# One load queue for the front of a decoder layer, and the cache compression spread over the input projection

## The chip, the cores and the metric

The kernel runs on one core of a Trainium2 chip. The core has a matrix engine (TensorE, PE in the profile), VectorE (DVE), ScalarE (ACT), GpSimd (POOL) and SyncE (SP). Each engine takes its instructions in program order; SP, ACT and POOL also issue DMAs, which run on 16 DMA engines. The metric is the device time of one execution in microseconds (us).

## The reference

One layer of a decoder, for a prompt of 1024 tokens and for 8 batches of 8 new tokens that have a cache of past keys and values. Cut to what matters:

```python
mod = (silu(c) @ w_ada + b_ada)[:, None, :]
shift1, scale1, gate1, shift2, scale2, gate2 = split(mod, 6)
h = rms_norm(x, norm1) * (1 + scale1) + shift1
z = h @ w_in
q, kc, vc, ks, vs, kw, vw, gates, conv_bg, conv_cg, conv_h, pool_in = split(z, IN_SPLITS)
...
k_cmp = rms_norm(compress(full[:, :, 0], cmp_pe[0], cmp_w1[0], cmp_w2[0]), k_gain[0])
v_cmp = compress(full[:, :, 1], cmp_pe[1], cmp_w1[1], cmp_w2[1])
...   # three attentions (compressed, selected, window), convolution, pooling
x = x + gate1 * (concat([o_attn, y_conv, y_pool]) @ w_out)
h = rms_norm(x, norm2) * (1 + scale2) + shift2
x = x + gate2 * swiglu(h, w_up, w_down)
```

Everything is fp32. `compress` turns overlapping blocks of the past keys and values into one row each, by two small matrices (`w1`, `w2`) and a position term (`pe`).

## The kernel before

Features lie on the 128 partitions, tokens along the free dimension: 1024 prompt tokens and 64 new ones, in three chunks of 384, 384 and 320 (`CHUNKS`, line 26). Products that need fp32 accuracy are three matmuls of a high and a low part (`mm3`, line 141).

The program is written as tasks: Python generators that emit a step and yield the time, by a rough clock of the engines, from which their next step can run (`run`, line 83). The order in which steps are emitted, with some freedom that the recording layer takes by a timeline of its own, fixes the order of every engine's queue. So a change of the tasks moves instructions on all engines. Waits are semaphores; a tile that is used again waits for its last readers.

The stages that the change touches:

- **Modulation** (`ada_rounds`, line 339). Six vectors (shift1, scale1, gate1, shift2, scale2, gate2), numbered 0 to 5. The weights of one vector come in 16 loads. Before, a round is half a vector: per step four loads of 256 KB, in pieces of 128 columns (512 B), and 16 matmuls of 128 columns on quarters of the array, accumulated over two steps, then an evacuation, a transpose and an add (line 380). Vectors 0 and 1 are made in the front, the other four (`late_ada`, line 899) during the input projection, with one step of loads ahead.
- **Norm** (`norm_load` 435, `norm_squares` 441, `modulate` 404). x comes by ScalarE's queue. Squares on ScalarE are summed over the eight feature tiles on VectorE into `n_ss`; one matmul with a matrix of 1/1024 (`mean_d`) makes the mean; then root (ScalarE) and reciprocal (VectorE, `n_rs`). Then, per feature tile, scale into a temporary `n_t`, add the shift into `h_hi` and form `h_lo`.
- **Compression** (`compress`, line 498). The cache pages come eight at a time, an octet (`compress_load`, 492: six by SP's queue and two by POOL's, into one of three `stream` tiles, one of which holds `w1`). One octet is 16 fp32 matmuls of 128 columns. Four octets are a batch; `compress_evac` and `compress_post` (575) close it with a few small matmuls (`vt,c_w`, `ksq,mean_h`, a transpose of `vcT`). The first three batches (`EARLY`) run in this stage, the other five in the attention. `compress_prompt` (549) does the same for the prompt's own keys.
- **Input projection** (`input_projection`, line 833). First the token part (`token_part`, 672): nine token tiles by the 280 columns of `wtok` (vs, vw, gates), with eight loads of `wtok` on ScalarE's queue and low parts on VectorE. Then 16 weight tiles by three chunks, 48 steps of 24 matmuls.

The front runs as one task (`front`, line 1920) at priority 1, next to the input projection at 1 and the compression at 2 (line 1986); the compression fills the time in which the other two wait. After the projection come the attention, the output projection and the feed-forward part, in which no line changes but for the names of two tiles.

Of the kernel before, what the change touches and what calls it, by code (L numbers as in the profile page):

```python
# [17 lines left out]
P = 128  # L18
# [3 lines left out]
NB = 8  # L22
# [38 lines left out]
class Kernel:  # L61
# [55 lines left out]
    def bank_of(self, tag):  # L117
        """waits for a bank of the tag"""
        while not self.free[tag] or min(self.free[tag]) > self.t["pe"]:
            yield self.ready(tag)  # L120
        return self.take(tag)

    # ---------------------------------------------------------------- helpers
    def mm(self, out, lhsT, rhs, start, stop, chain=False):
# [10 lines left out]
        self.nc.tensor.matmul(out, lhsT, rhs, start=start, stop=stop, skip_group_check=chain)  # L135
# [5 lines left out]
    def mm3(self, out, a, b, start, stop, chain=False):  # L141
        self.mm(out, a[0], b[0], start, False, chain)
        self.mm(out, a[0], b[1], False, False, chain)
        self.mm(out, a[1], b[0], False, stop, chain)
# [10 lines left out]
    def combine(self, out, a, b, op, n, ready=0.0, eng=None):  # L155
        """out = a op b in SBUF on VectorE or GpSimd, by default the one that is done first"""
# [25 lines left out]
    # ---------------------------------------------------------------- constants  # L182
# [60 lines left out]
    def constants3(self, c):  # L243
        nc = self.nc
        with self.pool("ctmp") as tp:
# [9 lines left out]
            # zeros, then the causal triangle; the window's older edge; the compressed blocks that are not over yet  # L255
# [15 lines left out]
            # row index -> token t of a sample row (b2, g, r, t)  # L271
# [7 lines left out]
            # sum over the four heads of a key group  # L279
# [12 lines left out]
            # new tokens: key (b', t') is seen by row (b, t) when b' == b and t' <= t  # L292
# [11 lines left out]
            # the oldest window keys: key k is out of the window of token t when k <= t  # L304
# [6 lines left out]
            # token partition (64 + (b, t)) -> row (b2, g, r, t) of the pair p  # L311
# [8 lines left out]
            # head of a sample row  # L320
# [10 lines left out]
    # ---------------------------------------------------------------- adaLN  # L331
# [7 lines left out]
    def ada_rounds(self, pool, rs, bufs, eng, tag, margin=0.0):  # L339
        """vectors rs of the modulation, [feature, (prompt, 8 batches)], half a vector at a time"""  # L340
        nc = self.nc
        todo = [(r, hf) for r in rs for hf in range(2)]
        steps = [(x, kh) for x in range(len(todo)) for kh in range(2)]
        W = {}

        def load(i):
            if i < len(steps):
                x, kh = steps[i]
                r, hf = todo[x]
                W[i] = []  # L350
                for g in range(4):
                    t = pool.tile([P, KT // 2, P], F32, name="wada", bufs=bufs)
                    eng.dma_start(t, self.i["wada"][r * 4 + g, :, kh * 4:kh * 4 + 4, hf * P:(hf + 1) * P])
# [5 lines left out]
        for i in range(ahead):  # L359
            load(i)  # L360
        for i, (x, kh) in enumerate(steps):
            r, hf = todo[x]
            yield W[i][4] + margin
            if kh == 0:
# [7 lines left out]
            if kh == 0:  # L372
                continue
            s = pool.tile([P, P], F32, name="ada_s", bufs=2)
            r_ = self.evac(s, acc[:, :P], P)
# [3 lines left out]
            self.tr(tr[:, :P], s)  # L379
            nc.vector.tensor_tensor(  # L380
                self.mod[:, r].rearrange("p (g j) b -> p j g b", j=2)[:, hf],
                tr[:, :P].rearrange("p (g m) -> p g m", m=32)[:, :, 0:9],
                self.bada[:, r].rearrange("p (g j) -> p j g", j=2)[:, hf][:, :, None].to_broadcast([P, 4, 9]),
                op=OP.add)
            self.give(tag, self.use("dve", 0.2, self.t["pe"]))
            if hf == 1:
                if r in (1, 4):
                    out, norm = (self.s1, self.norm1) if r == 1 else (self.s2, self.norm2)
                    nc.vector.scalar_tensor_tensor(out, self.mod[:, r], 1.0, norm[:, :, None].to_broadcast([P, KT, 9]),
                                                   op0=OP.add, op1=OP.mult)  # L390
                self.ada_at[r] = self.use("dve", 0.3, self.t["pe"]) + 0.2
# [1743 lines left out]
```

## Time and profile before

| | us |
|---|---|
| timed runs: median of 3 (lowest, highest) | 1712.49 (1708.04, 1713.7) |
| profiled execution, first to last instruction (span) | 1707.9 |
| TensorE busy | 1606.5 (94%) |
| VectorE busy | 1121.0 (66%) |
| ScalarE busy | 821.8 (48%) |
| GpSimd busy | 704.6 (41%) |

The profiled execution is one execution, taken by the hardware profiler; its span lies just under the lowest timed run. In the profile's rows L135 is the helper that records every matmul, so matmuls are told apart by their operands: `bank<-wada,sc` is the modulation, `bank<-stream` the compression, `bank<-wt_hi,h_hi` and the like the token part, `bank<-h_hi,w_hi` the projection. "PE" is the matmul, "PEld" its weight load. Idle time is given with what released it.

### The profile page before, as it was taken

What the parts mean: (1) busy time and instruction counts of PE and PEld (TensorE: products, weight loads), DVE (VectorE), ACT (ScalarE), POOL (GpSimd) and SP (SyncE); (2) the same over time, 40 slices, a digit from 0 to 9 for tenths busy, and PEclk for the clock granted to TensorE, in tenths of its full rate; (3) what the DMA queues carried; (4) which work ended last, traced back from release to release, by engine and by line L of the source; (5) the groups of instructions that cost most, each with busy time, mean ns of one, the idle gap of its engine ahead of it and who ended that gap; (6) DMA issues with size and microseconds to landing.
All of it is one profiled execution on the core that took longest, in us unless ns stands there. A gap on an engine that the chain in (4) does not pass through costs nothing.

```text
span 1707.9 us, 35277 instructions
## 1 busy us (share of the span) xinstructions
PE 1606.5 (94%) x12317; PEld 1427.7 (84%) x12317; DVE 1121.0 (66%) x2886; ACT 821.8 (48%) x1892; POOL 704.6 (41%) x812
## 2 busy tenths in 40 slices
PE   6789999997999999999799789999999999899998
PEld 5689999987877566666599779999999998889997
DVE  1491334767556867666599996555555556998887
ACT  1363212326676766766675543332333334655554
POOL 1121000003342322222206486555555555888976
PEclk9899999999999999999999989999999999999999
DMA  9854455425664644540883224225222225744433
GB/s 273 258 180 127 143 141 138 136 75 179 202 193 128 195 141 122 160 131 10 276 253 105 75 72 135 96 96 194 97 96 100 96 96 186 237 128 130 133 82 125
DMA packets 214851, 245.13 MB, mean 144 GB/s; under 512 B 25985, under 2 KB 182850, under 8 KB 214354
## 3 DMA queue, kind: packets, MB, share of 16 engines
q1 hardware_dynamic: 190546, 209.77, 40.1%
q10 hardware_dynamic: 18288, 17.01, 3.2%
q0 software_dynamic: 5840, 16.10, 2.9%
q8 instruction: 98, 1.61, 0.4%
q14 instruction: 79, 0.65, 0.1%
HBM read 202.33 MB, written 44.67 MB: 145 GB/s over the span
## 4 chain that ended last, share of the span: by engine, by line
PE 31%; DVE 9%; issue 4%; DMA 3%; POOL 3%; ACT 1%; ACTq 0%; POOLq 0%; DVEq 0%; SPq 0%
PE bank L135 31%; DVE w_lo L160 2%; DMA w_raw<-in_wup 2%; POOL w_s L160 1%; DVE b_lo L160 1%; DVE g_lo L160 1%; DVE x L1706 1%; DVE d_lo L160 1%; POOL b_t L160 1%; DMA w_raw<-in_wdown 0%; DMA mixc<-mix_d 0%; ACT w_hi L164 0%; DMA x<-x_d 0%; DVE n_ss L160 0%; POOL f_T L160 0%
## 5 line engine op out<-in xcount | busy, mean ns | idle before, releaser
L135 PE MATMUL bank<-b_lo,w_hi 128*128 128x272 f32 x1232 | 355.8, 291 | 2.7 <-DVE b_lo L160 2.5
L135 PE MATMUL bank<-b_hi,w_hi 128*128 128x272 f32 x1232 | 351.6, 292 | 6.9 <-DVE f_v L1512 3.3
L135 PE MATMUL bank<-b_hi,w_lo 128*128 128x272 f32 x1232 | 351.4, 290 | 2.1 <-DVE w_lo L160 2.1
L135 PEld LDWEIGHTS bank<-b_hi,w_hi 128*128 128x128 f32 x1232 | 232.1, 191 | 9.6 <-ACT b_hi L164 4.9
L135 PEld LDWEIGHTS bank<-b_lo,w_hi 128*128 128x128 f32 x1232 | 234.5, 190 | 4.0 <-DVE b_lo L160 3.9
L135 PEld LDWEIGHTS bank<-b_hi,w_lo 128*128 128x128 f32 x1232 | 233.0, 190 | 3.1 <-DVE w_lo L160 2.8
L160 POOL TENSOR_TENSOR w_s<-w_raw 128x512 f32<-128x512 f32 (+1 forms) x122 | 164.2, 1347 | 147.8 <-DVE w_lo L160 134.1
L1011 POOL TENSOR_SCALAR P<-P,st 128x640 f32<-128x640 f32 (+11 forms) x192 | 111.5, 591 | 241.8 <-DVE st L1009 89.5
L164 ACT ACTIVATE w_hi<-w_raw 128x512 fp32r<-128x512 f32 (+2 forms) x130 | 86.5, 676 | 176.5 <-PE bank L135 141.2
L160 DVE TENSOR_TENSOR w_lo<-w_raw,w_hi 128x512 fp32r<-128x512 f32 (+2 forms) x129 | 115.6, 904 | 83.2 <-PE bank L135 47.4
L160 DVE TENSOR_TENSOR w_lo<-w_s,w_hi 128x512 fp32r<-128x512 f32 (+1 forms) x144 | 127.4, 888 | 45.4 <-ACT w_hi L164 38.6
L135 PE MATMUL bank<-stream 128*128 128x128 f32 x1056 | 137.2, 289 | 19.4 <-DMA stream<-in_cacheA 14.5
L135 PEld LDWEIGHTS bank<-stream 128*128 128x128 f32 x1056 | 130.4, 203 | 28.5 <-issue 21.8
L160 POOL TENSOR_TENSOR x<-x,d_m 128x272 f32<-128x272 f32 x144 | 141.1, 1001 | 25.2 <-DVE x L1706 13.1
L164 ACT ACTIVATE w_hi<-w_s 128x512 fp32r<-128x512 f32 (+1 forms) x144 | 89.2, 624 | 113.2 <-PE bank L135 57.1
L135 PE MATMUL bank<-h_hi,w_hi 128*128 128x384 f32 (+1 forms) x384 | 129.4, 337 | 1.0 <-ACT py L826 1.0
L135 PE MATMUL bank<-h_hi,w_lo 128*128 128x384 f32 (+1 forms) x384 | 126.7, 330 | 0.0
L135 PE MATMUL bank<-h_lo,w_hi 128*128 128x384 f32 (+1 forms) x384 | 126.4, 329 | 0.0
L1003 ACT ACTIVATE P<-P,st 128x640 f32<-128x640 f32 (+11 forms) x192 | 113.0, 591 | 13.0 <-DVE st L994 6.5
L135 PE MATMUL bank<-g_hi,w_hi 128*128 128x272 f32 x308 | 92.0, 301 | 13.1 <-DVE x L1706 6.7
L139 PEld LDWEIGHTS bank<-ident,P 128*128 128x128 f32 (+1 forms) x592 | 64.1, 138 | 46.4 <-issue 30.2
L139 PE MATMUL bank<-ident,P 128*128 128x128 f32 (+1 forms) x592 | 95.6, 284 | 2.5 <-DVE pt L152 1.7
(363 smaller groups left out, 4111.0 us busy)
## 6 DMA issues: line engine op xcount, KB each, us to landing
wada<-in_wada SPq DMA_DIRECT2D x96, 256.0 KB, 5.2
stream<-in_cacheA SPq DMA_DIRECT2D x192, 128.0 KB, 3.1
w_raw<-in_wup SPq DMA_DIRECT2D x48, 512.0 KB, 3.9
g_raw<-g_d SPq DMA_DIRECT2D x70, 272.0 KB, 3.1
unit<-in_cacheB SPq DMA_DIRECT2D x136, 128.0 KB, 2.3
stream<-in_cacheB SPq DMA_DIRECT2D x120, 128.0 KB, 2.2
w_raw<-in_wout SPq DMA_DIRECT2D x24, 512.0 KB, 4.5
g_d<-f_T SPq DMA_DIRECT2D x84, 136.0 KB, 1.8
```

The source lines that it names most:

```text
L135: self.nc.tensor.matmul(out, lhsT, rhs, start=start, stop=stop, skip_group_check=chain)
L139: self.nc.tensor.transpose(out, in_, self.ident)
L160: (self.nc.vector if eng == "dve" else self.nc.gpsimd).tensor_tensor(out, a, b, op=op)
L164: self.nc.scalar.activation(hi, src, AF.Copy)
L1003: nc.scalar.activation(Ps, Ps, AF.Exp, scale=-1.0, bias=sy[:, 0:1], accum_out=sy[:, 1:2])
L1011: nc.gpsimd.tensor_scalar(Ps, Ps, sy[:, 3:4], 0.0, op0=OP.mult, op1=OP.add)
L1706: nc.vector.scalar_tensor_tensor(out[:, :n], acc[:, :n], self.mod[:, 5, m, 0:1], out[:, :n], op0=OP.mult, op1=OP.add)
```

## The change

SP's queue brings, in this order: x's first chunk, the 16 loads of scale1, x's second chunk, the token weights in two loads, the 16 loads of shift1, x's last chunk, then `w1` and cache pages. A load of modulation weights now takes two feature tiles by whole rows of 256 columns (2 KB in one piece per partition); a modulation matmul is 256 columns wide, and a vector is accumulated over four steps. The order of the two vectors is scale first, then shift.

For the first two chunks the mean is taken on TensorE from each feature tile's squares (eight matmuls, no sums on VectorE); the last chunk keeps the sums. x is scaled in place as soon as the scale vector is there, and the shift is added in a second pass; the new tokens' part is done for all feature tiles at once. x's second chunk lies in the tile that later takes the projected keys and values. The token weights lie in two `stream` tiles, and GpSimd forms their low parts.

The compression starts behind the token tile that ends the second chunk, and its priority is now 0.9 while octets x 30 < 12 x steps of the projection, else 2: its twelve octets are spread over the projection's first 30 steps.

```diff
     def ada_rounds(self, pool, rs, bufs, eng, tag, margin=0.0):
-        todo = [(r, hf) for r in rs for hf in range(2)]
-        steps = [(x, kh) for x in range(len(todo)) for kh in range(2)]
+        steps = [(r, kq) for r in rs for kq in range(4)]
...
-                    t = pool.tile([P, KT // 2, P], F32, name="wada", bufs=bufs)
-                    eng.dma_start(t, self.i["wada"][r * 4 + g, :, kh * 4:kh * 4 + 4, hf * P:(hf + 1) * P])
+                    t = pool.tile([P, 2, 256], F32, name="wada", bufs=bufs)
+                    self.ada_load = eng.dma_start(t, self.i["wada"][r * 4 + g, :, kq * 2:kq * 2 + 2, :])
...
-        for i in range(ahead):
-            load(i)
+        with self.tc.issue_after(self.x_load.ins):
+            for i in range(ahead):
+                load(i)
...
-            for k in range(4):
+            for k in range(2):
                 for g in range(4):
-                    self.mm(acc[32 * g:32 * g + 32, :P], self.sc[:, kh * 4 + k, :], W[i][g][:, k, :],
-                            kh + k == 0, kh + k == 4)
+                    self.mm(acc[32 * g:32 * g + 32, 0:256], self.sc[:, kq * 2 + k, :], W[i][g][:, k, :],
+                            kq + k == 0, kq + k == 4)
...
+    def norm_load(self, c, x):
+        c0, n = CHUNKS[c]
+        self.x_load = self.nc.sync.dma_start(x, self.i["xT"][:, :, c0:c0 + n])
...
+    def norm_scale(self, pool, c, rs, x, r, tag="b"):
...
+        if c == 2:
+            ss = pool.tile([P, 384], F32, name="n_ss")
+            for k in range(KT):
+                r = self.square_sum(pool, ss, x[:, k, :n], k, n, r)
...
+        else:
+            m = yield from self.bank_of(tag)
+            for k in range(KT):
+                sq = pool.tile([P, 384], F32, name="n_t", bufs=2)
+                nc.scalar.activation(sq[:, :n], x[:, k, :n], AF.Square)
...
+                self.mm(m[:, :n], self.mean_d, sq[:, :n], k == 0, k == KT - 1)
...
+    def modulate(self, c, x, hi, lo, at):
...
+        for k in range(KT):
+            t = x[:, k, :np_]
+            nc.vector.scalar_tensor_tensor(t, t, s[:, k, 0:1], rs[:, :np_], op0=OP.mult, op1=OP.mult)
...
+        yield from self.hold(lambda: 0 in self.ada_at and (c == 0 or c - 1 in self.h_done))
...
+            nc.scalar.activation(hk, t, AF.Identity, bias=sh[:, k, 0:1])
...
+            nc.vector.scalar_tensor_tensor(lk, t, sh[:, k, 0:1], hk.bitcast(F32), op0=OP.add, op1=OP.subtract)
...
     def compress_setup(self, pool):
-        nc.sync.dma_start(w1, self.i["w1"].rearrange("p v k m -> p (v k) m"))
-        for x in range(2):
-            self.compress_load(x)
+        with self.tc.issue_after(self.x_load.ins):
+            nc.sync.dma_start(w1, self.i["w1"].rearrange("p v k m -> p (v k) m"))
+            for x in range(2):
+                self.compress_load(x)
...
     def compress(self, pool, batches, ahead):
-        yield from self.hold(lambda: self.ada_loaded >= 5)
+        yield from self.hold(lambda: self.tok_last)
...
+    def token_loads(self):
+        for half in range(2):
+            raw = self.stream_tile().rearrange("p a b -> p (a b)")[:, 0:1120].rearrange("p (k m) -> p k m", k=4)
+            self.nc.sync.dma_start(raw, self.i["wtok"][:, half * 4:half * 4 + 4])
...
     def token_part(self, pool, h):
+            r = self.split(hi[:, s], lo[:, s], raw, 1120, at, "pool")
...
+            if j == 5:
+                self.tok_last = last
...
     def input_projection(self, h):
-        yield from self.hold(lambda: self.ada_done)
+        yield from self.hold(lambda: self.ada_loaded >= 8)
...
     def front(self, h):
+        def begin(pool, c, x):
+            rs = pool.tile([P, 384], F32, name="n_rs", bufs=2)
+            xs[c] = self.norm_load(c, x())
+            self.spawn(0.4 + 0.1 * c, self.norm_scale(pool, c, rs, *xs[c]))
+            self.spawn(0.4 + 0.1 * c, self.modulate(c, xs[c][0], h[c][0], h[c][1], self.h_at[c]))
...
-                ada = self.ada_rounds(ap, (0, 1), 16, self.nc.sync, "b")
+                begin(np_, 0, lambda: np_.tile([P, KT, CHUNKS[0][1]], F32, name="x0"))
+                ada = self.ada_rounds(ap, (1, 0), 16, nc.sync, "b")
+                t = next(ada)
+                x1 = self.kv.rearrange("p v t -> p (v t)")[:, 0:KT * CHUNKS[1][1]]
+                with self.tc.issue_after(self.ada_load.ins):
+                    begin(np_, 1, lambda: x1.rearrange("p (k t) -> p k t", k=KT))
+                    self.token_loads()
...
+                with self.tc.issue_after(self.ada_load.ins):
+                    begin(n2, 2, lambda: n2.tile([P, KT, CHUNKS[2][1]], F32, name="x2"))
...
     def build(self):
-        self.run((1, self.front(h)), (1, self.input_projection(h)), (2, self.compress(cp, range(EARLY), 1)))
+        early = lambda: 0.9 if self.octets * 30 < EARLY * 4 * self.z_steps else 2
+        self.run((1, self.front(h)), (1, self.input_projection(h)), (early, self.compress(cp, range(EARLY), 1)))
```

`issue_after(x)` keeps what is emitted under it behind x on its engine; `hold` waits with the emission until a condition holds. Comments that the diff drops are left out here.

More of the change, by code (lines that the diff above doesn't have):

```diff
@@ L134, in mm @@
         self.t["pe"] += cost
-        self.nc.tensor.matmul(out, lhsT, rhs, start=start, stop=stop, skip_group_check=chain)
+        return self.nc.tensor.matmul(out, lhsT, rhs, start=start, stop=stop, skip_group_check=chain)
     def tr(self, out, in_):
@@ L378, in ada_rounds @@
             tr = yield from self.bank_of(tag)
[L379 to L391, printed above, removed]
+            for j in range(2):
+                self.tr(tr[:, j * P:(j + 1) * P], s[:, j * P:(j + 1) * P])
+            for j in range(2):
+                nc.vector.tensor_tensor(
+                    self.mod[:, r].rearrange("p (g j) b -> p j g b", j=2)[:, j],
+                    tr[:, j * P:(j + 1) * P].rearrange("p (g m) -> p g m", m=32)[:, :, 0:9],
+                    self.bada[:, r].rearrange("p (g j) -> p j g", j=2)[:, j][:, :, None].to_broadcast([P, 4, 9]),
+                    op=OP.add)
+            self.give(tag, self.use("dve", 0.4, self.t["pe"]))
+            if r in (1, 4):
+                out, norm = (self.s1, self.norm1) if r == 1 else (self.s2, self.norm2)
+                nc.vector.scalar_tensor_tensor(out, self.mod[:, r], 1.0, norm[:, :, None].to_broadcast([P, KT, 9]),
+                                               op0=OP.add, op1=OP.mult)
+            self.ada_at[r] = self.use("dve", 0.3, self.t["pe"]) + 0.2
     def square_sum(self, pool, ss, x, k, n, ready, width=384, eng="dve"):
@@ L449, in compress_setup @@
+        self.h_done.add(c)
     def compress_setup(self, pool):
@@ L676, in token_part @@
         lo = pool.tile([P, KT, 280], F32R, name="wt_lo")
-        for k in range(KT):
-            raw = pool.tile([P, 280], F32, name="wt_raw", bufs=3)
-            nc.scalar.dma_start(raw, self.i["wtok"][:, k])
-            r = self.split(hi[:, k], lo[:, k], raw, 280, self.use("dma", 0.45, self.t["pe"]) + 2)
+        yield from self.hold(lambda: self.wt_raw)
+        for half, (raw, at) in enumerate(self.wt_raw):
+            s = slice(half * 4, half * 4 + 4)
+            yield at
+            r = self.split(hi[:, s], lo[:, s], raw, 1120, at, "pool")
         yield r
@@ L1964, in build @@
         self.cmp_done = self.heads = self.v_done = self.u_done = 0
-        self.ada_done = False
+        self.ada_done = self.x_loaded = False
         self.ada_loaded = 0
+        self.wt_raw = []
+        self.tok_last = None
         self.constants()
```

131 lines of the change are left out of this document (61 added, 70 removed).

## The prediction

> **What bounds the kernel now.** I read first the windows of busy time, cut where the kernel's stages change: up to the first matmul of the token part, up to the last of the input projection, the attention, and all that follows. The columns are TensorE (PE), its weight loads, VectorE, ScalarE, GpSimd, the granted clock, the DMA share and GB/s.
>
> ```profile
> 0.00:113.16 113.16, 82.81 (x674) 69.35 (x675) 53.35 (x132) 42.06 (x94) 19.83 (x43) 0.92 0.83 248
> 113.16:382.66 269.50, 265.48 (x2030) 249.71 (x2028) 126.23 (x199) 75.95 (x136) 22.21 (x40) 1.00 0.45 129
> 382.66:832.64 449.98, 432.46 (x3270) 297.31 (x3271) 303.14 (x1437) 311.22 (x804) 138.75 (x252) 0.99 0.50 153
> 832.64:1707.90 875.26, 825.79 (x6348) 811.32 (x6347) 638.25 (x1121) 392.60 (x860) 523.77 (x479) 0.97 0.41 130
> ```
>
> From 113 us on TensorE is the bound: it idles 4.0 us of 269.5 in the projection and 17.5 of 450 in the attention. Only the first 113 us have room: 30 us idle, and a part of the busy time runs slowly. So a change of the front is worth what it does to two sums: when the dense stretch starts, and how much work it then holds.
>
> The timeline of TensorE shows where the stretch begins and ends, and what fills the time before it (start, length, instruction, records; an fp32 matmul leaves two records; in brackets the idle time and its releaser).
>
> ```profile
> 36.72 6.06 PE L135 MATMUL bank<-stream 128*128 128x128 f32 x32
> 45.18 0.64 PE L135 MATMUL bank<-wada,sc 128*32 128x128 f32 x2 [2.40 <-DMA wada<-in_wada]
> 45.74 0.80 PE L135 MATMUL bank<-stream 128*128 128x128 f32 x2
> 46.47 0.64 PE L135 MATMUL bank<-wada,sc 128*32 128x128 f32 x2
> ...
> 50.50 1.92 PE L135 MATMUL bank<-wada,sc 128*32 128x128 f32 x26
> ...
> 56.63 1.95 PE L135 MATMUL bank<-wada,sc 128*32 128x128 f32 x64
> ...
> 59.15 1.46 PE L135 MATMUL bank<-n_ss,mean_d 128*128 128x384 f32 x4
> ...
> 88.55 3.74 PE L135 MATMUL bank<-stream 128*128 128x128 f32 x32
> ...
> 113.16 0.37 PE L135 MATMUL bank<-wt_hi,h_hi 128*128 128x280 f32 x1
> ...
> 115.81 3.73 PE L135 MATMUL bank<-stream 128*128 128x128 f32 x32
> 119.30 0.37 PE L135 MATMUL bank<-wt_hi,h_lo 128*128 128x280 f32 x1
> ...
> 381.85 0.81 PE L135 MATMUL bank<-h_sq,mean_h 128*128 128x320 f32 x2 [0.42 <-ACT h_sq L705]
> ```
>
> The reader is to see that nearly all of the compression (bank<-stream, 32 records for eight pages, an octet) runs ahead of the token part. It is the filler under the front's transfers, and moving it costs what it takes later.
>
> **What the change moves behind the start.** The groups of the first 140 us, by shape (busy us, mean ns):
>
> ```profile
> L135 PE MATMUL bank<-stream 128*128 128x128 f32 x384 | 53.6, 303 | 13.0 <-DMA stream<-in_cacheA 12.1 <-DVE n_t L429 0.9
> L135 PE MATMUL bank<-c_peT,stream 128*128 128x2 f32 x32 | 7.0, 352 | 2.7 <-DMA stream<-in_w 2.7
> L135 PE MATMUL bank<-vt,c_w 64*64 64x256 f32 x24 | 2.5, 487 | 2.2 <-ACT vt L579 2.2
> L135 PE MATMUL bank<-ksq,mean_h 128*128 128x256 f32 x6 | 1.8, 379 | 0.0
> L139 PE MATMUL bank<-ident,vcT 128*128 128x128 f32 x6 | 1.1, 272 | 0.0
> ```
>
> 384 records are 12 octets; one lies behind 113.16 already, at 115.81. In the changed program all 12 stand behind the token part or inside the projection, so 11 are added. One takes 119.30 - 115.81 = 3.49 us: 38.4. The position term (c_peT) moves with them: 7.0, or 3.5 at the rate of the octet's records (3.49/32 each); I take 7.0 as measured. Two of the three closing steps (the last three rows, 5.4/3 = 1.8 each) are added: 3.6. The third chunk's statistics, half of the row at 59.15, move too: 0.7. Sum 49.7. The late modulation matmuls are half as many and twice as wide, the same columns: 0.
>
> **When the stretch can start.** SP's queue now brings x's first chunk, the scale vector's 16 loads, x's second chunk, the token weights, then the shift vector's 16 loads. By the issue rows:
>
> ```profile
> wada<-in_wada SPq DMA_DIRECT2D x96, 256.0 KB, 5.2
> x<-in_xT ACTq DMA_DIRECT2D x2, 1536.0 KB, 17.3
> wt_raw<-in_wtok ACTq DMA_DIRECT2D x8, 140.0 KB, 4.7
> ...
> 16.00:20.00 4.00, 2.93 (x34) 1.74 (x32) 0.09 (x2) 0.00 (x0) 0.00 (x0) 1.00 1.20 291
> 24.00:28.00 4.00, 2.72 (x33) 1.80 (x33) 0.20 (x1) 0.28 (x1) 0.00 (x0) 1.00 0.99 382
> 32.00:36.00 4.00, 4.00 (x20) 4.00 (x20) 0.01 (x1) 0.98 (x3) 0.00 (x0) 1.00 1.07 367
> ```
>
> That is 32 x 256 + 2 x 1536 + 1120 KB = 12,384 KB, 12.7 MB. While only the half rows of wada (512 B a piece) flow the engines are full at 291 GB/s; while x, w1 and cache pages (1 KB and more) flow, at 367 to 382. Whole rows are 2 KB, so I take 370: 34 us from about 2.5 us, the last landing near 38. At 291 it would be 46.
>
> TensorE's share of this stage: 64 modulation matmuls of 256 columns and 16 statistics matmuls straight from the squares (before: 3, with 21 sums on VectorE). Their price depends on the clock. The same 32 records take 6.06 us at 36.72 and 3.74 at 88.55, though the clock column says 1.00 for both: the early one ran at nearly half speed. The Trainium skill, TensorE: Matmul & The Clock Gate, Part 1, says the idle default is half the clock and that about 3.4 us of sustained work lifts it; the trace agrees in kind, but its first 30 us of thin work did not lift it. By that rule alone the clock would be full from 12 us on, the first vector's stage end at 23 and the token part start near 45 instead of 47, as the second half's transfers then set the pace. A modulation matmul of 128 columns costs 1.92/13 = 0.148 us slow (50.50) and 1.95/32 = 0.061 fast (56.63), so one of 256 takes 0.30 or 0.12; a statistics matmul 1.46/2 = 0.73 fast, 1.46 slow. The built program mixes the two kinds: for the first vector eight runs of one beside the other. Alternation at 45.18 to 46.47 takes 1.29 us a pair, where 0.148 and 6.06/16 = 0.38 would be 0.53; so 0.76 a pair, 6 us for eight, half of it fast. The Trainium skill, TensorEngine Tiling (Array Packing), Key Properties, gives the reason: a change of tiling mode drains the array, which speaks against this mixing; the row has its price. Each vector's stage is then 3.8 + 5.8 + 3 = 12.7 us fast or 9.6 + 11.7 + 6 = 27.3 slow.
>
> x's first chunk lands near 8.5. I assume slow until 20 and fast then, as the work is now nearly unbroken: the first vector ends at 20 + (1 - 11.5/27.3) x 12.7 = 27.4. Some 9 us later, with the transposes 10, the second chunk's last statistics are through. In the built order VectorE then has the second chunk's reciprocal and eight scalings ahead of the shift's add:
>
> ```profile
> L413 DVE RECIPROCAL n_rs<-n_rs 128x384 f32<-128x384 f32 x2 | 5.0, 2524 | 2.0 <-ACT n_rs L410 2.0
> L423 DVE SCALAR_TENSOR_TENSOR h_lo<-n_t,mod,h_hi 128x384 fp32r<-128x384 f32 x16 | 9.7, 614 | 0.8 <-ACT h_hi L421 0.7
> 113.36 1.68 DVE L423 SCALAR_TENSOR_TENSOR h_lo<-n_t,mod,h_hi 128x384 fp32r<-128x384 f32 x3
> ```
>
> 37.5 + 0.7 + 2.5 + 8 x 0.56 (1.68/3) = 45.2, and about 1.5 more for the root, the add and the first h: the token part starts at 47. Bounds: 42 if the transfers alone set it (38, then 4 us from the landing to h), 65 if every matmul is slow (8.5 + 54.6 + 2).
>
> Behind the start I add 5.5 us of new stalls: the first token tile waits for eight h_lo at 0.56 us, 4.5 where its 24 matmuls need 3.2 (20 of them between 113.16 and 115.81), 1.3; the third chunk's statistics, which stand in TensorE's order ahead of the second chunk's tiles, wait for ScalarE's squares behind 16 h_hi, 1.5 to 2; entering and leaving an octet costs 3.74 - 3.49 = 0.25, 2.6 for eleven. Bounds 2 and 15. The input weights' loads stand behind x's last chunk, w1 and two octets on SP; the token part's 28 us cover them, and without that cover the first tile would be some 10 us late. GpSimd forms the token weights' low parts (two of 1,120 columns, by the row below 1347 ns x 1120/512 = 2.9 each) ahead of its first cache pages; both are through by 37, ten us before they are due. ScalarE loses the eight wtok issues and x's issues; it is no bound here (76 of 269.5 us).
>
> ```profile
> L160 POOL TENSOR_TENSOR w_s<-w_raw 128x512 f32<-128x512 f32 (+1 forms) x122 | 164.2, 1347 | 147.8 <-DVE w_lo L160 134.1
> ```
>
> **The sum.** 47 + 269.5 + 49.7 + 5.5 = 371.7 against 382.7: 11 us earlier. The attention does the same work in a slightly other order, the rest in nearly the same; I carry the gain through, with 3 us either way. The profiled execution spans 1707.9, the three runs lie at 1708.0 to 1713.7 with a median of 1712.5. 1707.9 - 11 = 1697 in span, 1701.5 on the median's scale.
>
> **The rivals.**
> Half clock: the mixed stage never keeps TensorE full enough to lift the clock. For it speaks that everything before 41 us ran slowly; against it that the statistics use the whole array without waiting. Start at 65: 389.7, 7 later, 1719.5. It decides from a start of 58 on.
> Late octets: pages and weights share SP's in-order queue with modulation loads that wait for TensorE, so each octet waits, now inside the dense stretch.
>
> ```profile
> PE bank L135 <- DMA stream<-in_cacheA: 12.1, 4, 4.9
> 200.63 2.70 SPq L353 DMA_DIRECT2D wada<-in_wada  x4
> 203.38 0.49 SPq L639 DMA_DIRECT2D w_raw<-in_win  x1
> ```
>
> At 12.1/4 = 3 us for 12 octets it is 36 us: 1737.5; slower from 1 us each. Against it: twelve octets are paced over 30 of the 48 projection steps, which share the stretch at some 5 us each, so one is due about every 13 us, and its loads are issued one octet ahead.
> Wide rows bring nothing: 291 GB/s as before, landing at 46, start at 50 or 51, gain 7: 1705. The Trainium skill, DMA: Bandwidth & Descriptors, Specifications, puts line rate at 512 B and above, which would leave the half rows at line rate already; the windows at 16 and 24 us contradict it so far.
> The attention gives it back: its 17.5 us of idle grow with the other order: 1712.
> Better: start at 42, position term 3.5, stalls 2: 22 us, 1690.5.
>
> **How the numbers follow.** Forecast 0.46 (its own range 1697 to 1706), half clock 0.16, late octets 0.10, narrow rate 0.12, given back 0.08, better 0.08. 0.3% is 5.1 us, about what a measurement of this kernel can tell from no change. Faster: nearly all of the forecast, the better case and two thirds of the narrow rate, 0.60. Slower: the late octets and half of the half clock, 0.18, as its start may lie anywhere from 55 to 65. The remaining 0.22 is no change. The range leaves out the late octets' end and the far end of the better case: 1692 to 1718.
>
> **What would show it.** First token matmul at 44 to 50 us in the timeline; GB/s of the first 38 us near 370; the last projection matmul near 372; octets of 3.5 to 3.8 us without a DMA in front; VectorE's eight scalings just ahead of the shift's add. A start above 55 with slow records tells for the half clock; TensorE waiting for cache pages or wada between 90 and 370 us for late octets.

## The result, and the profile after

The changed kernel took 1705.25 us (median of 11 runs, 1700.11 to 1712.24), the kernel before beside it 1712.49 (11 runs): 0.9961 of it, 95% interval 0.9948 to 0.9975, 7 us. The forecast was 11. A second comparison (in the experiments, e9) gave 1705.61 against 1707.56, 0.9994 with 0.9978 to 1.0009. The changed kernel's medians agree; the kernel before lay at 1712.49, 1708.43, 1710.54 and 1707.56 in four sets of runs, which were not all on one chip, so times from different sets are compared by their ratios to it. The two intervals do not overlap; together they allow anything from no gain to 9 us, with medians 2 to 7 us apart. What follows goes by the traces, where the stages can be told apart.

The windows of the changed kernel, cut at the first token matmul, the last matmul of the projection and the first of the output projection (columns as in the prediction):

```profile
0.00:44.42 44.42, 29.29 (x165) 10.55 (x165) 20.41 (x36) 15.45 (x27) 13.83 (x23) 1.00 0.97 344
44.42:368.38 323.96, 318.78 (x2183) 295.30 (x2184) 146.22 (x243) 98.50 (x184) 33.68 (x60) 0.98 0.48 147
368.38:836.30 467.92, 439.96 (x3296) 300.57 (x3295) 311.48 (x1440) 317.22 (x821) 139.78 (x253) 0.98 0.51 153
836.30:1704.60 868.30, 821.06 (x6320) 808.11 (x6320) 635.47 (x1114) 386.68 (x848) 519.65 (x479) 0.98 0.40 127
```

The same last two windows of the kernel before, cut at the same instructions:

```profile
382.66:842.97 460.31, 436.48 (x3296) 299.15 (x3296) 305.98 (x1445) 316.28 (x816) 138.75 (x252) 0.99 0.51 156
842.97:1707.90 864.93, 821.76 (x6320) 809.48 (x6320) 635.40 (x1114) 387.55 (x848) 523.77 (x479) 0.97 0.40 128
```

Read as sums: the start is 68.7 us earlier, the dense stretch 54.5 longer, so the projection ends 14.3 earlier. The attention then takes 7.6 longer for the same 3296 matmul records: 3.5 more of busy time (slower records) and 4.1 more idle. What is left at the output projection is 6.7. (The prediction's window of the attention ended at 832.64, ten microseconds short of the first matmul of the output projection, so TensorE's idle time there is 23.8 us and not 17.5.) The last stage took 3.4 more in this pair; no line of it is changed, and over all the profiles of this study it scatters from 861 to 868 us with no order in it, so nothing is read from it.

The front in the changed kernel, by windows of 4 us:

```profile
8.00:12.00 4.00, 1.64 (x3) 0.56 (x4) 0.84 (x6) 0.52 (x1) 0.70 (x2) 1.00 1.02 345
12.00:16.00 4.00, 4.00 (x15) 1.15 (x18) 0.26 (x1) 1.46 (x3) 0.00 (x0) 1.00 1.05 381
20.00:24.00 4.00, 4.00 (x28) 1.43 (x22) 0.00 (x0) 2.05 (x3) 0.00 (x0) 1.00 1.07 380
24.00:28.00 4.00, 3.17 (x17) 1.25 (x16) 2.96 (x5) 3.24 (x6) 0.23 (x1) 1.00 1.03 405
```

and its TensorE timeline:

```profile
12.93 1.65 PE L135 MATMUL bank<-n_t,mean_d 128*128 128x384 f32 x2
15.10 0.91 PE L135 MATMUL bank<-n_t,mean_d 128*128 128x384 f32 x2
...
25.86 0.41 PE L139 MATMUL bank<-ident,ada_s 128*128 128x128 f32 x2 [0.56 <-ACT ada_s L150]
...
40.62 1.05 PE L135 MATMUL bank<-wada,sc 128*32 128x256 f32 x10 [0.22 <-DMA wada<-in_wada]
42.15 0.44 PE L139 MATMUL bank<-ident,ada_s 128*128 128x128 f32 x2 [0.47 <-ACT ada_s L150]
44.42 0.39 PE L135 MATMUL bank<-wt_hi,h_hi 128*128 128x280 f32 x1 [1.84 <-ACT h_hi L459]
56.87 0.81 PE L135 MATMUL bank<-n_ss,mean_d 128*128 128x320 f32 x2 [1.39 <-DVE n_ss L160]
```

From 8 to 28 us the transfers run at 345 to 405 GB/s. A statistics matmul takes 1.65 us at 12.93 and 0.91 at 15.10: there TensorE's clock went up, although the clock column has 1.00 for both windows. The last modulation load is waited for until 40.62, and the transposes that follow it end at 42.59.

The end of the projection is where the two kernels part. First the changed one, then the kernel before:

```profile
368.21 7.31 PE L135 MATMUL bank<-stream 128*128 128x128 f32 x64
378.67 5.47 PE L135 MATMUL bank<-stream 128*128 128x128 f32 x32 [3.15 <-DMA stream<-in_cacheA]
388.19 0.53 PE L135 MATMUL bank<-kh,qs 128*128 128x192 f32 x1 [4.06 <-DVE qs L983]
```

```profile
386.05 9.04 PE L135 MATMUL bank<-stream 128*128 128x128 f32 x64 [3.39 <-DVE q L714]
397.08 3.81 PE L135 MATMUL bank<-stream 128*128 128x128 f32 x32 [2.00 <-DMA stream<-in_cacheA]
400.65 0.34 PE L135 MATMUL bank<-kh,qs 128*128 128x192 f32 x1
```

In both, three octets are all that TensorE has until VectorE has made the keys' and queries' parts. From the projection's end to the first score matmul it is 19.8 us in the changed kernel and 18.0 before. The octet at 378.67 takes 5.47 us, where 3.81 is the full speed: the granted clock is 1.00 in the wait ahead of it and 0.69 over the octet, and the first score matmul is slow as well (0.53 against 0.34). The kernel before loses some clock here too: 0.81 over its two octets at 386.05, behind the wait of 3.39.

### The profile page after: what moved, and what is told of

Read it like the earlier page. It is cut to its first block, busy times and chain, and to the rows that moved or that the text cites. A ratio compares the mean times of both kernels' runs of the same rounds, so it can differ in the third digit from the quotient of the medians.

```text
span 1704.6 us, 34455 instructions
## 1 busy us (share of the span) xinstructions
PE 1609.1 (94%) x11961; PEld 1414.5 (83%) x11961; DVE 1113.6 (65%) x2830; ACT 817.8 (48%) x1878; POOL 706.9 (41%) x814
## 5 line engine op out<-in xcount | busy, mean ns | idle before, releaser
L1050 POOL TENSOR_SCALAR P<-P,st 128x128 f32<-128x128 f32 (+12 forms) x192 | 112.0, 592 | 259.2 <-DVE st L1048 86.3
L1042 ACT ACTIVATE P<-P,st 128x128 f32<-128x128 f32 (+12 forms) x192 | 113.2, 591 | 28.4 <-DVE st L1033 13.8
L1033 DVE CUSTOM_DVE_ANT_0 P<-bank,m_slc 128x256 f32<-128x256 f32 (+5 forms) x136 | 68.1, 513 | 54.2 <-PE bank L135 29.2
```

The source lines that it names most:

```text
L1033: nc.vector.tensor_tensor_reduce(out=Pt[:, h, col:col + n], in0=S[:, p0:p0 + n], in1=mk, scale=-1.0, scalar=3e38, op0=OP.add, op1=OP.min, ...
L1042: nc.scalar.activation(Ps, Ps, AF.Exp, scale=-1.0, bias=sy[:, 0:1], accum_out=sy[:, 1:2])
L1050: nc.gpsimd.tensor_scalar(Ps, Ps, sy[:, 3:4], 0.0, op0=OP.mult, op1=OP.add)
```

## The experiments

**Rows of 512 bytes again (e1).** The front's 32 loads of modulation weights go back to half vectors; order and queue stay.

```diff
-                    t = pool.tile([P, 2, 256], F32, name="wada", bufs=bufs)
-                    eng.dma_start(t, self.i["wada"][r * 4 + g, :, kq * 2:kq * 2 + 2, :])
+                    t = pool.tile([P, KT // 2, P], F32, name="wada", bufs=bufs)
+                    eng.dma_start(t, self.i["wada"][r * 4 + g, :, kh * 4:kh * 4 + 4, hf * P:(hf + 1) * P])
```

> Only the shape of the front's 32 modulation loads is undone: pieces of 512 B per partition again (half a vector at a time), in the changed order and on the same queue. Theory (row width sets when the last landing comes, and the landing sets the start): 32 x 256 KB are 8.39 MB; at the 291 GB/s that the kernel before showed while only half rows flowed they take 28.8 us, at the 380 of the changed kernel's windows 22.1. First token matmul 6 to 8 us later, near 51, projection end near 375, time 5 to 8 us above the changed kernel, so about that of the kernel before. Rival (VectorE's eight scalings set the start, the landing is hidden behind them): start within 2 us of 44.4, time within 2 us.

1710.23 us, 1.0013 of the kernel before (0.9998 to 1.0028): 5 us above the changed kernel's medians, 3 to 9 us by the ratios. Windows of its front:

```profile
12.00:16.00 4.00, 3.10 (x9) 1.19 (x8) 0.32 (x1) 1.46 (x3) 0.00 (x0) 1.00 1.22 285
16.00:20.00 4.00, 4.00 (x42) 2.04 (x40) 0.00 (x0) 1.04 (x2) 0.00 (x0) 1.00 1.21 290
24.00:28.00 4.00, 2.19 (x39) 1.18 (x38) 2.67 (x3) 0.86 (x2) 0.00 (x0) 1.00 1.06 377
```

and the first token matmul:

```profile
50.81 0.58 PE L135 MATMUL bank<-wt_hi,h_hi 128*128 128x280 f32 x1
```

The theory holds: 285 to 303 GB/s from 12 to 24 us, while the half rows flow, 377 while x does, and a start 6.4 us later. With half rows the landing sets the start: TensorE waits for the last load until 48.39, 7.8 us later than in the changed kernel, and the matmuls behind it run at a low clock (0.50 granted from 48 to 52 us). In the changed kernel the landing is no longer the last to come: the transposes end at 42.59, and VectorE's add for them stands behind its eight scalings until 43.53 (the rows are under e12). The projection ends at 371.22 and not near 375, 2.6 to 5.1 us after the executions with whole rows.

**The spreading alone (e2).** The kernel before, with the compression held behind the sixth token tile and paced as in the change.

```diff
-        yield from self.hold(lambda: self.ada_loaded >= 5)
+        yield from self.hold(lambda: self.tok_last)
...
-        ..., (2, self.compress(cp, range(EARLY), 1)))
+        ..., (lambda: 0.9 if self.octets * 30 < EARLY * 4 * self.z_steps else 2, self.compress(cp, range(EARLY), 1)))
```

> The kernel before with one part of the change: the compression starts behind the sixth token tile and is spread over 30 projection steps; loads, norm and modulation stay as before. Theory (two halves are needed: the filler must go, and the loads must be put in order): before, SP issued stream loads from 23.5 to 42.0 us between the wada loads, so without them the modulation ends some 17 us sooner, at 42 to 45 instead of 59, and root, reciprocals and h take some 13 us more: first token matmul at 55 to 62. The dense stretch grows by the same 50 to 55 us as in the changed kernel: projection end at 375 to 386, where the kernel before had 382.7, and the time within 5 us of the kernel before. Rival (moving the filler is the whole gain): start below 50, projection end below 372, time 6 us or more under the kernel before. Rival (the loads are the whole gain, the spreading costs): time 6 us or more above the kernel before.

1728.3 us, 1.0125 (1.0108 to 1.0143): 20 us slower. By its time the third outcome held; the figures for the start (55 to 62) and for the projection's end (375 to 386) were missed:

```profile
66.49 1.41 PE L135 MATMUL bank<-n_ss,mean_d 128*128 128x320 f32 x2 [14.73 <-DVE n_ss L160]
67.23 0.90 PE L135 MATMUL bank<-wt_hi,h_hi 128*128 128x280 f32 x1
```

TensorE stands idle for 14.7 us: the third chunk's statistics are ahead of the first token tile in its queue, and wait for sums that VectorE makes between other work. The projection ends at 390.1, 7.4 us after the kernel before. That is less than half of the 20. The attention took 469.6 us, 9.2 more than in the kernel before: e2 has the changed kernel's order there, which e6 below prices at 5 to 7.5 us with the old front. So the filler's removal brings no gain unless the front's chain is shortened too, but in the stages that it touches it costs 7 us and not 20. The new loads with the filler left in the front were not run.

**No spreading (e3).** The changed kernel with `early = 2`.

> The changed kernel without the pacing: the early compression keeps priority 2, so by the order of the program one octet stands before the projection, one at its 40th step and eleven behind its end. Theory (the pacing puts 38 us of TensorE work where its pages are long there): projection end 38 us earlier, near 330, then eleven octets whose pages (1 MB each, 2.8 us at the 375 GB/s of this core's fullest windows, 3.8 at 277) come no faster than TensorE uses them, in a stretch that shows TensorE idle for pages 5 to 12 us in all; their closings come last and delay the keys. Time 4 to 12 us above the changed kernel. Rival (where the octets stand is of no account): within 2 us. Rival (octets at the end hide VectorE's tail of the projection, which left TensorE idle 8.8 us between 368 and 408): 3 us or more faster.

1724.49 us, 1.0097 (1.0081 to 1.0112), 19 us above the changed kernel, more than expected. TensorE's waits from the projection's end (325.18) to the first score matmul (404.46), in us in total, times, longest:

```profile
PE bank L135 <- DMA stream<-in_cacheA: 10.2, 5, 2.8
PE bank L135 <- ACT stream L150: 4.9, 1, 4.9
PE bank L135 <- DVE pre L538: 4.5, 1, 4.5
```

Pages cost what was expected; the closing of the prompt's own compression, with nothing beside it, adds 9.4 that the expectation had not priced. The first score matmul comes 16.3 us after the changed kernel's (388.19). The order behind it is another one as well, so the 19 us are not those waits alone.

**Sums on VectorE (e4).** `if c == 2:` becomes `if True:` in `norm_scale`, so that all chunks have one statistics matmul; the squares' temporary `n_t` of these sums has two buffers instead of three.

> The changed kernel with the squares of the first two chunks summed on VectorE again, one statistics matmul a chunk, so that TensorE no longer changes between 32-column and 128-column matmuls. Theory (start set by the last landing near 40.6 us, or by VectorE's work of the second chunk, whichever is later): VectorE gets 14 sums of about 0.55 us, half of them beside the first chunk's scalings; second chunk's reciprocal 2 to 5 us later than 36.7, first token matmul at 46 to 50, time 1 to 5 us above the changed kernel. Rival (the change of tile shape costs TensorE enough to set the start): start 2 us or more below 44.4 and the time lower. Rival (without the full-width matmuls TensorE's clock is not lifted, the modulation matmuls stay at the slow 0.30 us to the end): start at 50 or later.

1721.81 us, 1.0077 (1.0058 to 1.0095), with a start at 61.76 where 46 to 50 was expected. TensorE:

```profile
44.65 0.44 PE L139 MATMUL bank<-ident,ada_s 128*128 128x128 f32 x2 [0.53 <-ACT ada_s L150]
60.99 1.43 PE L135 MATMUL bank<-n_ss,mean_d 128*128 128x320 f32 x2 [15.91 <-DVE n_ss L160]
61.76 0.90 PE L135 MATMUL bank<-wt_hi,h_hi 128*128 128x280 f32 x1
```

The shift vector is transposed at 44.65, 2.5 us after the changed kernel (42.15), and VectorE's add for it came at 47.53, so a start near 48.5 was in reach, as the theory has it; the other 13 us are those of e2 again, the third chunk's statistics ahead of the first token tile. It does not show what the change of tile shape costs: the records of the modulation cannot be compared where the clock differs. In the changed kernel the same matmul stands behind three token tiles and waits 1.39 us (the row at 56.87). The attention, in the changed kernel's order, took 475.1 us here, 5 to 8 more than in any other kernel with that order; why is open.

**The order of the attention (e5, e6, e7, e9, e10).** The attention's instructions are emitted in an order that follows the planner's rough clock. At its start the clock of VectorE stood 4.49 us ahead of TensorE's in the changed kernel and 4.99 before; e1, e2, e4 and e12 have the changed kernel's order too. One line sets it:

```diff
+        self.t["dve"] = self.t["pe"] + 4.99
         hp_.__exit__(None, None, None)
```

> The changed kernel with one number of the planner set: its rough clock of VectorE at the start of the attention is 4.99 us ahead of TensorE's, as in the kernel before, where the changed kernel had 4.49. With it TensorE's order in the attention is that of the kernel before again, instruction by instruction; front and projection are untouched. So far the attention (projection end to the first matmul of the output projection) took 460.3 us in the kernel before and 467.9, 470.0 and 469.5 in three kernels whose order is the changed kernel's. Theory (the order alone gives back 8 us of the front's gain): attention 459 to 463, time 6 to 9 us under the changed kernel, 0.991 to 0.993 of the kernel before. Rival (the attention is longer because of what comes before it, late pages or VectorE's tail): attention 467 to 470, time within 2 us of the changed kernel.

> The mirror: the kernel before with 4.49 us in that place, which gives it the changed kernel's order in the attention and leaves its front and projection. Theory (the order alone): attention 467 to 470, time 6 to 10 us above the kernel before. Rival (what comes before it): attention 460, time within 2 us.

> The changed kernel with 4.00 us in that place: a third order of the attention, neither that of the kernel before nor that of the changed kernel. If each order has a price of its own, this one may take anything from 458 to 475 us, and neither theory can say which; if the length is set by what comes before the attention, it takes 467 to 470 and the time is that of the changed kernel within 2 us.

> The changed kernel once more, beside the two variants below on one chip, to set the size of the order's share directly. If order alone cost 2 us in the changed kernel (attention 467.9 with its order, 465.9 with that of the kernel before), it comes out 1 to 4 us above the 4.99 us clock's ratio of 0.9956, at 0.996 to 0.998; projection end at 368 to 369, attention 467 to 470.

> The kernel before once more, for a second profile: if the 460.3 us of its attention is no chance of one execution, it lies within 2 us of that again, with no single wait of TensorE above 4 us near the projection's end; if the profiles scatter by as much as the kernels differ, it comes out at 464 or more.

| kernel | attention's order | attention, us | time, us | of the kernel before |
|---|---|---|---|---|
| before; again (e10) | own | 460.3; 462.7 | 1707.56 to 1712.49 | 1 |
| before, 4.49 (e6) | changed | 467.8 | 1714.78 | 1.0025 (1.0009 to 1.0041) |
| changed; again (e9) | own | 467.9; 469.9 | 1705.25; 1705.61 | 0.9961; 0.9994 |
| changed, 4.99 (e5) | before | 465.9 | 1702.06 | 0.9956 (0.9938 to 0.9975) |
| changed, 4.00 (e7) | a third | 474.6 | 1710.40 | 1.0000 (0.9985 to 1.0016) |

The windows of e6, e10 and e5 that carry this:

```profile
382.76:850.57 467.81, 440.44 (x3296) 301.58 (x3296) 308.69 (x1440) 317.28 (x821) 139.32 (x252) 0.98 0.51 153
```

```profile
381.22:843.96 462.74, 439.31 (x3296) 301.17 (x3296) 306.87 (x1445) 316.19 (x816) 138.77 (x252) 0.98 0.51 155
```

```profile
368.51:834.37 465.86, 440.88 (x3297) 302.04 (x3296) 309.32 (x1445) 316.63 (x816) 138.71 (x253) 0.97 0.51 153
```

Each order has a price: with the kernel before's front, the changed order adds 5.1 to 7.5 us to the attention and 4 to the time; the third order adds 9 to the attention of e5 and 8 to its time. But the exchange is not symmetric. Given back its old order, the changed kernel's attention gets only 2 to 4 us shorter, and stays 3 to 6 above the kernel before. The theory that the order alone took the 8 us is not borne out by e5; behind the old front, by e6, it would account for nearly all of it. The times missed their forecasts too: e5 was to gain 6 to 9 us, e6 to lose 6 to 10 and lost 4, e9's ratio lay above its 0.996 to 0.998, and e10's attention between its two marks.

The windows split the difference. In the old order (before, e10, e5) TensorE idles 23.8, 23.4 and 25.0 us of the attention, in the changed order 27.4 to 28.5 (e6, after, e9, and e12 alike; e1, e2 and e4, with other fronts, 31 to 33). So some 3 to 4 us of idle time go with the order. The rest is busy time of the same records. In the old order it is 436.5, 439.3 and 440.9 us, and it follows the clock: over the first 120 us behind the projection the granted clock is 0.97, 0.94 and 0.91. The kernel before's first profile is the fast one of the three, and its second differs from e5 by hardly more than from the first. That the new front makes the old order longer is therefore not shown.

Where e5 loses its time can be placed by the score matmuls, which now come in one order in both kernels: e5 leads the kernel before (first profile) by 14.2 us at the projection's end, 12.4 at the first score matmul, 10.8 up to the latter's 489 us, 6.6 from its 495 us on, then about 6 to 800, and 8.6 at the output projection. Two stretches, two waits:

```profile
378.05 3.84 PE L135 MATMUL bank<-stream 128*128 128x128 f32 x32 [2.40 <-DMA stream<-in_cacheA]
388.27 0.53 PE L135 MATMUL bank<-kh,qs 128*128 128x192 f32 x1 [6.38 <-DVE qs L983]
...
481.79 2.49 PE L135 MATMUL bank<-stream 128*128 128x128 f32 x16 [2.44 <-DMA stream<-in_cacheA]
```

```profile
478.51:488.51 10.00, 7.57 (x45) 5.66 (x44) 4.45 (x33) 5.04 (x20) 3.82 (x10) 0.83 0.58 180
```

Over the ten microseconds that begin with the wait of 2.44 us the granted clock is 0.83, and the lead shrinks by 4.2. The kernel before has no wait there. SP asks for the last of its six pages of that octet at 477.87 in e5 and at 486.64 in the kernel before, which less the lead of 10.83 would be 475.81: e5 asks 2.1 us late. One of the six requests held SP's queue for 1.63 us, where the others took 0.33. Why it did is open.

**Mask instructions on GpSimd (e8).** `nc.vector` becomes `nc.gpsimd` for the copies and most `tensor_scalar` of `constants3`, on top of e5.

> The kernel of the 4.99 us clock, and 16 of VectorE's small instructions that form masks at the start of the attention go to GpSimd; TensorE's order differs in a few places near the start. In the changed kernel VectorE works without a gap from 367 to 390 us, and the first score matmul waits 4.06 us for its qs; these instructions sum to 3.3 us of that stretch. Theory (VectorE's chain sets the first scores): first score matmul 2 to 4 us sooner after the projection's end than in the kernel without this edit, time 2 to 4 us lower. Rival (TensorE waits for the next link, pages or the closing of a batch): within 1 us. Rival (two VectorE instructions now wait for GpSimd's slower ones, ahead of qs): 1 to 4 us slower.

1704.33 us, 0.9967 (0.9952 to 0.9983), 2 us above e5. The first score matmul comes 18.5 us after the projection's end, where e5 has 19.8: 1.3 sooner, not 2 to 4. The order near the start changed with it, one octet went behind the first scores, and the attention took 468.6. No gain, and no clean test.

**Three octets loaded (e11).** The last argument of the early compression becomes 0, on top of e5.

> The kernel of the 4.99 us clock, with no octet loaded ahead of need at the end of the early compression: the tiles then rotate so that three octets, not two, can lie loaded when the projection ends. TensorE's order in the attention becomes a fourth one. Theory (behind the projection TensorE lacks loaded pages: it waited 2.40 us for pages and 6.38 for qs there, and ran slowly for 30 us after): three octets run without a wait, TensorE's idle time from the projection's end to the first score matmul falls from 8.8 us to 5 or less and the time by 2 to 5 us below the 4.99 us clock's. Rival (VectorE's chain ends no sooner and the wait only moves): first score matmul again 19 to 20 us after the projection's end, time within 2 us of it; the new order can add or take up to 8 us by itself, as the third order did, so the idle time and the first score matmul decide, and the total only with them.

1709.01 us, 1.0004 (0.9989 to 1.0020). The edit did not do what was meant. SP's queue:

```profile
374.08 2.94 SPq L517 DMA_DIRECT2D stream<-in_cacheA  x6
```

The third octet's pages are asked for 3.6 us behind the projection's end (370.48), as ever, and TensorE waits 2.50 us for them and 6.15 for qs. What three loaded octets are worth was not tried. What it does give is a fourth order with an attention of 473.9 us.

**Low parts on VectorE (e12).** `"pool"` becomes `"dve"` in the token weights' split.

> The changed kernel with the token weights' low parts on VectorE instead of GpSimd. Theory (the two engines slow each other when both run two-input operations in SBUF): the first chunk's eight scalings take 0.54 us each, as the second chunk's do, where they took 1.10 beside GpSimd's 5.4 us; two additions of some 1.2 us each come after them, the second chunk's reciprocal starts when its statistics are done, 35.5 to 36.5 us, and the first token matmul within 1.5 us of 44.4. Rival (the scalings are slow for their operands): 1.10 us each again.

One time, 1703.31 us. First the changed kernel's VectorE (the first row is cut at two of the eight scalings), its GpSimd, then e12's VectorE:

```profile
27.97 5.65 DVE L452 SCALAR_TENSOR_TENSOR x<-x,s,n_rs 128x384 f32<-128x384 f32 x2
27.97 8.82 DVE L452 SCALAR_TENSOR_TENSOR x<-x,s,n_rs 128x384 f32<-128x384 f32 x8
36.72 2.54 DVE L432 RECIPROCAL n_rs<-n_rs 128x384 f32<-128x384 f32 x1
39.29 4.32 DVE L452 SCALAR_TENSOR_TENSOR kv__93<-kv__93,s,n_rs 128x384 f32<-128x384 f32 x8
43.53 0.29 DVE L380 TENSOR_TENSOR mod<-bank,c_bada 128x36 f32<-128x36 f32 x2
```

```profile
27.77 5.44 POOL L160 TENSOR_TENSOR wt_lo<-stream,wt_hi 128x1120 fp32r<-128x1120 f32 x2 [18.59 <-ACT wt_hi L164]
```

```profile
31.18 4.33 DVE L452 SCALAR_TENSOR_TENSOR x<-x,s,n_rs 128x384 f32<-128x384 f32 x8
35.42 2.56 DVE L160 TENSOR_TENSOR wt_lo<-stream,wt_hi 128x1120 fp32r<-128x1120 f32 x2
39.50 2.55 DVE L432 RECIPROCAL n_rs<-n_rs 128x384 f32<-128x384 f32 x1 [1.52 <-ACT n_rs L429]
```

The scalings take 0.54 us each again, so it was GpSimd. In this execution TensorE's clock rose only at about 20 us instead of 15, everything of the first vector came 3 us later, and the start was 47.22, not within 1.5 us of 44.4; the reciprocal waited for its statistics, not for VectorE. In the changed kernel the root for that reciprocal ends at 36.66, just as the slowed scalings do. So they cost the start nothing that can be seen here.

## Why the prediction was right, point by point

**Transfers, 12.7 MB at 370 GB/s, last landing 38.** Right in rate (345 to 405), late by 2 to 3 us in the landing. e1 shows the price of the row width, 6.4 us of start and some 5 of time; the narrow-rate rival's start of 50 to 51 is what half rows gave. That rival's total, 1705, is the measured one, but only by chance: the start at 44.42 rules it out.

**TensorE at two speeds, slow until 20.** The clock rose at 15 us (12.93 to 15.10), and the first vector was through at 25.86, not 27.4. The half-clock rival fell. The rise moves from one execution to the next, 14 to 19 us in the five profiles of the same front (the changed kernel, e5, e7, e8, e9), and the start with it, 44.4 to 46.7, by way of the statistics, the reciprocal and the scalings; their projections end at 366.1 to 368.6 all the same, so part of a late start is made up in the stretch.

**The eight scalings ahead of the shift's add.** Right: 39.29 to 43.53, then the add. The start came at 44.42 against 47.

**Work moved behind the start, 49.7, and 5.5 of stalls.** The stretch grew by 54.5; the forecast's terms give 55.2. Its parts, by the groups of the stretch, after and before:

```profile
L135 PE MATMUL bank<-stream 128*128 128x128 f32 x418 | 52.0, 283 | 0.0
L135 PE MATMUL bank<-c_peT,stream 128*128 128x2 f32 x32 | 4.7, 281 | 0.0
```

```profile
L135 PE MATMUL bank<-stream 128*128 128x128 f32 x64 | 8.1, 276 | 0.0
```

354 records more, eleven octets, are 43.9 us, 4.0 each, where 3.49 and 0.24 for entry and exit had been taken: 2.9 too little. The position term is 4.7 instead of 7.0. No octet waited for a page inside the stretch, so the late-octets rival fell. The wait for the third chunk's statistics is 1.39, as forecast; that for h_lo did not show. The sum of the stretch is right because errors of 2 to 3 us cancel, which is luck.

**Carried through the attention, 3 us either way.** This is the step that failed. "The attention does the same work in a slightly other order" was priced at nothing; the attention took 7 us more (467.9 and 469.9 against 460.3 and 462.7), half of the 14.3 that the front had gained. The rival "the attention gives it back" had the place right and took it for the less likely case. Some 3 to 4 us of it are idle time that goes with the order. The rest is busy time of the same matmuls at a lower granted clock, and it depends on which profile of the kernel before is taken: its second has 2.8 us more of it than its first. In e5 the loss lies in the wait behind the projection and in one late octet, each made longer by the clock that falls with it. Two things stay open: why the changed order idles more, and whether the old order is longer behind the new front at all, as only the kernel before and the changed one were profiled twice.

That the total still fell within the forecast's own range, 1697 to 1706, is in part luck: the front came out 3 us better than forecast (368.4 against 371.7), the attention 5 to 10 us worse.

The version with the changed front and the old order (e5) has the lowest median, 1702.06, and the lowest ratio, 0.9956; its interval overlaps the changed kernel's.

## What to carry to other kernels

Work taken out of a wait is free only if the wait goes with it: with the filler alone removed the projection ended 7 us later, since the chain that it had covered was still there. Where a planner writes the order, an edit anywhere moves the order everywhere behind it; compare the orders, and give the later stage a price of its own (here 8 us of time between the best and the worst of four orders) instead of carrying a gain through it. Profile each side more than once before a difference of 3 us in one stage is explained. An in-order queue makes a small late instruction dear: one statistics matmul ahead of the first token tile kept TensorE waiting for 15 us, twice.

## What the runs showed of the hardware

**A VectorE instruction waits out a GpSimd instruction.** While GpSimd formed two low parts (5.44 us), VectorE finished two scalings (5.65 us), one for each; the other six took 0.53 each. In e4, seven sums beside the same two took 8.86 us. The prediction had priced GpSimd's work and not this. The Trainium skill, SBUF — State Buffer, SBUF: two separate sides, says that the pair of ports which the two share is locked for a whole instruction, not split, and names VectorE operations with two inputs in SBUF; the rows agree.

**Very thin matmuls can cost TensorE its clock, though it counts as busy.** The position term is 32 records of two columns:

```profile
77.14 4.68 PE L135 MATMUL bank<-c_peT,stream 128*128 128x2 f32 x32
```

```profile
80.00:84.00 4.00, 4.00 (x20) 4.00 (x21) 0.77 (x5) 0.00 (x0) 0.00 (x0) 0.50 0.93 338
84.00:88.00 4.00, 4.00 (x23) 4.00 (x23) 0.00 (x0) 0.00 (x0) 1.05 (x2) 0.71 0.14 44
```

TensorE counts as busy for all of it, yet the granted clock is 0.50 from 80 to 84 us and 0.71 after, so the octet behind it runs slowly: 4.90 us for 22 records. It is not so every time. In e9, the same program, the clock stays at 1.00 there and the 22 records take 2.70; e4, e8 and e12 show no fall either, while e1, e2, e3, e5, e7 and e11 do. In the kernel before, where the clock had not yet risen, the same 32 records filled 6.95 us from 29.90 without raising it: the octet behind them still took 6.06. The price of such matmuls can be more than their own time; that they are the cause of the fall is inferred from its place and not shown by a run without them.
